# Scores of two blocks in one stretch, softmax written behind the older values, one PSUM tile for both streams

## The chip, the cores and the metric

The kernel runs on one core of one Trainium2 chip. The metric is the device time of one execution in microseconds, as the median of several runs. A core has four computing engines that run beside each other, each with a queue of its own: TensorE (PE, with its weight loads PEld), VectorE (DVE), ScalarE (ACT) and GpSimd (POOL). SyncE (SP) issues the DMAs. TensorE writes only to PSUM, of which a core has eight banks of 512 float32 values per partition; the kernel divides all eight among three kinds of buffers.

## The reference

Two layers over 1024 tokens of width 1024, each of the form x + rmsnorm(mixer(rmsnorm(x))). Layer 0 is a gated multi-scale retention with 8 heads. Layer 1 is a gated differential attention, 8 heads, which is where the change lies:

```python
def block(args):
    q_i, i = args
    q_chunk = (i * Q_BLOCK + jnp.arange(Q_BLOCK)) // CHUNK
    mask = key_chunk[None, :] <= q_chunk[:, None]
    sc = jnp.einsum('bqhtd,bkhtd->bhtqk', q_i.astype(jnp.float32), kf) * scale
    p = jax.nn.softmax(jnp.where(mask, sc, neg), axis=-1)
    w = p[:, :, 0] - lam * p[:, :, 1]
    return jnp.einsum('bhqk,bkhe->bqhe', w, vf)
```

Each head has two streams t of queries and keys, 64 wide each. A block of 128 queries sees the keys up to its own chunk of 64, so block b needs 128 (b + 1) keys, of which the upper half of the queries alone sees the last 64. The two softmaxes are combined with the weight lam, multiplied with the values (128 wide), normed per head, gated, projected and normed again.

## The kernel before, in words

Everything is float32 in and out. A product of two matrices is made of three matmuls (helper `mm3`, its matmul on L100): each factor is split into a rounded high part and a low remainder (`split`, L87 and L88, or L90 and L91 with a scale), and high x high, high x low and low x high are summed in PSUM.

Layer 0 runs first: projections, retention and an output product, until about 850 us of the span. Then come the gates of layer 1, then its 64 units of projection, 8 heads (h) of 8 chunks of 128 tokens (c). This main loop, index i = 8 h + c, is the place of the change. One step of it projects chunk c of head h to queries, keys and values: eight slabs s, three matmuls of 128x384 each (`gemm_piece`, tile `pg`). Between the slabs other work is written:

- `ahead`: weights of a later head are fetched and split (L90, L91; tile `wbh`), one slab in each of the steps c = 1 to 4 and four in step c = 7;
- at s = 4, `transpose_b` turns the previous chunk's rotated queries and keys (L582 on TensorE, then L87 and L88);
- behind the odd slabs s = 1, 3, 5, 7, one of the "pieces" that the generator `attend` yields, two steps late (`LAG`).

At the end of a step `rotate_b` applies the rotary angles (L571, L572 on DVE, L573 on POOL) and copies the values (L574 on ACT).

A unit of attention is one head and one block b. It passes through three functions in three successive steps:

- `scores`: for each 512 keys, three matmuls for each of the two streams (L596). Stream t uses the rows 64 t to 64 t + 63 of queries and keys, so these matmuls work on half of the array's height each and the two streams run as a pair. Then, in the same function, softmax: a memset that masks the last 64 keys (L602), a maximum (L603), both on DVE, an exponential with its sum on ACT (L604), and on DVE the reciprocal, the weight and the combination of the two streams (L606, L607, L609).
- `turn`: transposes of the combined weights, up to four into one PSUM buffer (L621), and a copy on ACT (L622); two pieces for more than 512 keys.
- `values`: two instructions of TensorE for each key block (L632), then ACT reads the sum out (L635) and squares it (L636), a reciprocal root follows (L105 on DVE, L106 on POOL), the product on POOL (L638), and a DMA stores the block (L639).

So a step that scores unit k also values unit k - 2 and turns unit k - 1, in the written order scores with softmax, values, turn, turn.

PSUM buffers come from three tags: `g`, two of one bank (projections and output products); `s2`, two of two banks (1024 values; one for each stream of a unit); `s`, two of one bank (transposes, turns and values in rotation). SBUF tag `k` has six buffers of 1024 values, for softmax weights (`pr`), turned weights (`wT`) and rows of the output product.

The order on each engine is not simply the written one: a planner takes instructions by priority in the written order among those that are ready by its own clock of the engines, gives out buffers, and puts in the waits. What it has ordered, each engine runs in turn.

Behind the main loop, the remaining pieces of `attend` are woven with the output product: four of its steps (three matmuls of 128x512 each, `out_gemm`) stand ahead of the last `transpose_b`; then each of the remaining pieces is followed by three more. `out_fetch(t)` reads block t of the attention back from DRAM, when its eight heads are stored, multiplies it with the gate (L672), and `out_turn` transposes it (L680).

Of the kernel before, what the change touches and what calls it, by code (L numbers as in the profile page):

```python
# [18 lines left out]
P = 128  # L19
D = 1024  # L20
S = 1024
NC = S // P
NS = D // P
H = 8
# [11 lines left out]
def yoco_kernel(ctx: ExitStack, tc: tile.TileContext, a: dict):  # L36
# [31 lines left out]
    def kt(shape, nm, dt=F32):  # L68
        return sbuf("k", shape, dt, nm)

    def sm(n):
        return sbuf("m", [P, n], F32, "m")
# [3 lines left out]
    def ps(tag, n=512):  # L76
        return psum.tile([P, n], F32, name=f"p{tag}_{next(uid)}", tag=tag, bufs=PB[tag])
# [327 lines left out]
    for i in range(H * NC):  # L405
        h, c = divmod(i, NC)
        if c == 0:
            wq, wg = w_next
        u = {"h": h, "c": c, "wg": wg, "pp": ps("s2", 1024)}
# [176 lines left out]
    def scores(u):  # L586
        h, b, nk = u["h"], u["b"], u["nk"]
        q, qs = groups[h, b // 4][0][:, 0], slice(b % 4 * P, b % 4 * P + P)
        sc = [ps("s2", 1024) for t in range(2)]
        for c0 in range(0, nk, 512):  # L590
            n = min(512, nk - c0)
            k = groups[h, c0 // 512][0][:, 1]
            for i, (ql, kl) in enumerate(((0, 0), (0, 1), (1, 0))):
                for t in range(2):
                    rows = slice(t * 64, t * 64 + 64)
                    nc.tensor.matmul(  # L596
                        sc[t][:, c0 : c0 + n], q[rows, ql, qs], k[rows, kl, 0:n], start=(i == 0), stop=(i == 2)
                    )
        nm, s_ = sm(2), sm(2)
        pr = [kt([P, D], f"pr{t}") for t in range(2)]  # L600
        for t in range(2):
            nc.vector.memset(sc[t][0:64, nk - 64 : nk], NEG)  # L602
            nc.vector.tensor_reduce(out=nm[:, t : t + 1], in_=sc[t][:, :nk], axis=AX.X, op=ALU.max, negate=True)  # L603
# [34 lines left out]
        nc.gpsimd.tensor_tensor(out=o[:, 1], in0=o[:, 0], in1=r.to_broadcast([P, P]), op=ALU.mult)  # L638
        nc.sync.dma_start(og2d[b * P : (b + 1) * P, h * P : (h + 1) * P], o[:, 1])  # L639

    def attend(blocks):

        blocks = [{"h": h, "b": b, "nk": (b + 1) * P} for h, b in blocks]
        a_, b_ = None, None
        for u in blocks + [None, None]:
            pieces = []
            if u:
                pieces.append(lambda: scores(u))
            if a_:
                pieces.append(lambda: values(a_))  # L650
            if b_:
                pieces.append(lambda: turn(b_, 0))
                if b_["nk"] > 512:
                    pieces.append(lambda: turn(b_, 1))
            yield pieces
            a_, b_ = b_, u


    wob = {}
# [64 lines left out]
                yield  # L724

    LAG = 2
    att = attend([(h, b) for h in range(H) for b in range(NC)])
    prev = None
    for i in range(H * NC):
        h, c = divmod(i, NC)  # L730
# [24 lines left out]
        load_wob(f, wt([P, D], "wobh"), wt([P, D], "wobl"))  # L755
    spare = xt([P, 512], "spare", F32)
    og_ = outs()
    for _ in range(4):
        next(og_)
    transpose_b(*prev)  # L760
    for step in att:
# [91 lines left out]
```

## Time and profile before

| what | us |
|---|---|
| median of 3 runs (1496.89 to 1499.78) | 1497.07 |
| the profiled execution | 1498.85 |
| its span, from first to last instruction | 1496.8 |
| TensorE busy | 1478.4 |
| VectorE busy | 787.2 |
| ScalarE busy | 629.3 |
| GpSimd busy | 269.9 |
| scores on TensorE (L596), first to last start | 937.0 to 1401.4 |

Rows of a profile name the line, the engine, the operation, the tile written and the tile read, the shape (rows x columns of the array for TensorE, partitions x elements), and a count. In a group's row the two numbers behind the bar are the busy time in us and the mean of one in ns, then the idle time of the engine just before and what ended it. A row of the timeline begins with the start in us from the first instruction and the length of the merged run in us. TensorE's matmuls overlap: the next starts before the modelled end of the one before, so a run is measured from start to start.

### The profile page before, as it was taken

How to read it: one execution, taken by the hardware profiler on the slowest of the kernel's cores; microseconds unless marked ns; L12 is line 12 of the kernel's file. 1: busy time of each engine (PE TensorE's matmuls, PEld its weight loads, DVE VectorE, ACT ScalarE, POOL GpSimd, SP SyncE). 2: the span in 40 equal slices, each digit the busy share in tenths (PEclk: the TensorE clock that was granted, in tenths of full speed). 3: DMA queues.
4: the chain of work that ended last, by engine and by line, in shares of the span. 5: the costliest groups of instructions: out<-in, count | busy, mean ns of one | idle time of the engine just before them, and what ended most of it. 6: DMA issues, size and time to landing. Idle time of an engine off the chain costs nothing.

```text
span 1496.8 us, 23855 instructions
## 1 busy us (share of the span) xinstructions
PE 1478.4 (99%) x8770; PEld 1296.9 (87%) x8770; DVE 787.2 (53%) x1991; ACT 629.3 (42%) x1611; POOL 269.9 (18%) x470
## 2 busy tenths in 40 slices
PE   9999999999999999999999999999999999999998
PEld 7889888989889898888888888988988988988786
DVE  5764635454545454541155502667567576577543
ACT  5642424242424332342244513556455566466421
POOL 1322222222122222200000000122222222222100
PEclk9999999999999999999999999999999999999999
DMA  7530303020211111253445522111011011013342
GB/s 259 169 113 15 95 15 99 15 89 22 81 33 56 58 65 53 71 180 105 141 159 179 183 71 79 31 36 52 12 52 52 10 52 48 15 64 139 122 166 98
DMA packets 71173, 125.63 MB, mean 84 GB/s; under 512 B 7697, under 2 KB 42385, under 8 KB 71057
## 3 DMA queue, kind: packets, MB, share of 16 engines
q1 hardware_dynamic: 70768, 123.85, 25.3%
q8 instruction: 69, 1.13, 0.3%
q14 instruction: 48, 0.39, 0.1%
q10 hardware_dynamic: 288, 0.26, 0.1%
HBM read 94.72 MB, written 29.36 MB: 83 GB/s over the span
## 4 chain that ended last, share of the span: by engine, by line
PE 86%; DVE 5%; ACT 3%; issue 2%; DMA 2%; POOL 0%; DVEq 0%; POOLq 0%; ACTq 0%; SPq 0%
PE pg L100 58%; PE ps L100 14%; PE ps L596 4%; PE ps L632 3%; PE ps L621 2%; DMA stg<-in_wa 1%; PE ps L304 1%; ACT pr L604 1%; DVE wbh L91 1%; PE ps L254 1%; PE ps L582 1%; DVE m L603 1%; DVE wq L91 0%; PE ps L238 0%; PE ps L680 0%
## 5 line engine op out<-in xcount | busy, mean ns | idle before, releaser
L100 PE MATMUL pg<-wq,xT 128*128 128x512 f32 x1512 | 378.5, 399 | 1.1 <-ACT xT L87 0.5
L100 PE MATMUL pg<-wbh,x2T 128*128 128x384 f32 x1536 | 334.9, 353 | 0.0
L100 PEld LDWEIGHTS pg<-wq,xT 128*128 128x128 f32 x1512 | 274.7, 188 | 55.6 <-ACT wq L90 1.1
L100 PEld LDWEIGHTS pg<-wbh,x2T 128*128 128x128 f32 x1536 | 256.2, 189 | 13.0 <-issue 9.3
L100 PE MATMUL ps<-wg,xT 128*128 128x256 f32 x1536 | 195.8, 283 | 0.1
L100 PEld LDWEIGHTS ps<-wg,xT 128*128 128x128 f32 x1536 | 189.4, 192 | 0.7 <-DVE wg L91 0.3
L106 POOL TENSOR_TENSOR m<-m,mhalf 128x1 f32<-128x1 f32 x144 | 79.9, 555 | 572.7 <-DVE m L105 485.2
L604 ACT ACTIVATE pr<-ps,m 128x256 f32<-128x256 f32 (+7 forms) x128 | 94.1, 738 | 90.9 <-DVE m L603 90.9
L221 POOL TENSOR_TENSOR a<-a 128x256 f32<-128x256 f32 x64 | 48.2, 753 | 327.7 <-DVE a L220 321.8
L603 DVE TENSOR_REDUCE m<-ps 128x1 f32<-128x256 f32 (+7 forms) x128 | 91.1, 753 | 0.0
L100 PE MATMUL pg<-wbg,x2T 128*128 128x512 f32 x384 | 88.4, 390 | 0.0
L90 ACT ACTIVATE r<-pg,tabA 128x256 fp32r<-128x256 f32 x63 | 29.7, 471 | 134.0 <-DVE a L220 133.9
L100 PEld LDWEIGHTS pg<-wbg,x2T 128*128 128x128 f32 x384 | 71.8, 188 | 14.8
L100 PEld LDWEIGHTS ps<-r,r 128*128 128x128 f32 x528 | 72.1, 190 | 7.3 <-ACT r L256 1.5
L255 DVE TENSOR_TENSOR a<-ps,tabA 128x128 f32<-128x128 f32 x64 | 18.6, 290 | 112.0 <-PE ps L254 111.3
L100 PE MATMUL ps<-r,r 128*128 128x256 f32 x528 | 74.8, 284 | 1.0 <-ACT r L256 0.7
L632 PE MATMUL ps<-v,wT 128*128 128x128 f32 x576 | 74.6, 275 | 0.2 <-DVE ps L602 0.2
L632 PEld LDWEIGHTS ps<-v,wT 128*128 128x128 f32 x576 | 73.2, 191 | 0.7 <-PE pg L100 0.5
L573 POOL TENSOR_TENSOR tabB<-tabB 128x256 f32<-128x256 f32 x64 | 49.6, 775 | 124.9 <-DVE tabB L572 124.7
L219 DVE TENSOR_TENSOR a<-pg,tabA 128x256 f32<-128x256 f32 x63 | 26.6, 423 | 79.2 <-PE pg L100 79.2
L256 ACT ACTIVATE r<-a 128x128 fp32r<-128x128 f32 x64 | 19.9, 310 | 107.8 <-DVE a L255 107.8
L100 PE MATMUL pg<-wo,oh 128*128 128x512 f32 x192 | 60.8, 398 | 1.1 <-ACT oh L87 1.1
(158 smaller groups left out, 2387.2 us busy)
## 6 DMA issues: line engine op xcount, KB each, us to landing
stw<-in_wa SPq DMA_DIRECT2D x56, 256.0 KB, 2.8
stb<-in_wbh SPq DMA_DIRECT2D x64, 192.0 KB, 2.4
xr<-in_x SPq DMA_DIRECT2D x16, 512.0 KB, 4.4
stg<-in_wa SPq DMA_DIRECT2D x32, 256.0 KB, 3.3
ogd<-a SPq DMA_DIRECT2D x64, 128.0 KB, 1.9
sto<-in_woa SPq DMA_DIRECT2D x16, 512.0 KB, 3.7
og<-ogd SPq DMA_DIRECT2D x16, 512.0 KB, 4.0
y0d<-y SPq DMA_DIRECT2D x8, 512.0 KB, 2.7
```

What stands on the lines that cost most here:

```text
L90: nc.scalar.activation(hi, src, AF.Copy, scale=scale)
L100: nc.tensor.matmul(out, l, r, start=(first and i == 0), stop=(last and i == n - 1))
L106: nc.gpsimd.tensor_tensor(out=out, in0=t, in1=mhalf[:, 0:n], op=ALU.pow)
L219: nc.vector.tensor_tensor(out=o4(t1), in0=q4, in1=cb, op=ALU.mult)
L221: nc.gpsimd.tensor_tensor(out=qk, in0=t1, in1=t2, op=ALU.add)
L256: nc.scalar.activation(ss[:, 0, :], sc, AF.Copy)
L573: nc.gpsimd.tensor_tensor(out=r[:, 2], in0=r[:, 0], in1=r[:, 1], op=ALU.add)
L596: nc.tensor.matmul(sc[t][:, c0 : c0 + n], q[rows, ql, qs], k[rows, kl, 0:n], start=(i == 0), stop=(i == 2))
L603: nc.vector.tensor_reduce(out=nm[:, t : t + 1], in_=sc[t][:, :nk], axis=AX.X, op=ALU.max, negate=True)
L604: nc.scalar.activation(pr[t][:, :nk], sc[t][:, :nk], AF.Exp, bias=nm[:, t : t + 1], accum_out=s_[:, t : t + 1])
L621: nc.tensor.transpose(pt[:, k - k0 : k - k0 + P], w[:, k : k + P], ident)
L632: nc.tensor.matmul(po, wT[:, kb * P : (kb + 1) * P], v[:, kb % 4], start=(kb == 0), stop=(kb == b))
```

## The change

Score matmuls and softmax become two functions. The generator no longer walks over units but over 66 steps: within a head, steps 0 and 2 score nothing, step 1 scores blocks 0 and 1 one after the other, step 3 blocks 2 and 3, and steps 4 to 7 one block each. The softmax of the units just scored is written in the second piece, behind the values of older units; units scored together are turned together in the next step and valued together in the one after. A unit of up to 512 keys takes one `s2` buffer in place of two, stream 0 in the first 512 columns and stream 1 in the last, and likewise one `k` buffer for its softmax weights. Behind the main loop six steps of the output product in place of four stand ahead of the last `transpose_b`.

```diff
     def scores(u):
         h, b, nk = u["h"], u["b"], u["nk"]
         q, qs = groups[h, b // 4][0][:, 0], slice(b % 4 * P, b % 4 * P + P)
-        sc = [ps("s2", 1024) for t in range(2)]
+        if nk > 512:
+            sc = [ps("s2", 1024) for t in range(2)]
+        else:
+            both = ps("s2", 1024)
+            sc = [both[:, t * 512 : t * 512 + 512] for t in range(2)]
         for c0 in range(0, nk, 512):
...
+        u["sc"] = sc
+
+    def softmax(u):
+        nk, sc = u["nk"], u["sc"]
         nm, s_ = sm(2), sm(2)
-        pr = [kt([P, D], f"pr{t}") for t in range(2)]
+        if nk > 512:
+            pr = [kt([P, D], f"pr{t}") for t in range(2)]
+        else:
+            both = kt([P, D], "pr")
+            pr = [both[:, t * 512 : t * 512 + 512] for t in range(2)]
         for t in range(2):
             nc.vector.memset(sc[t][0:64, nk - 64 : nk], NEG)
...
-    def attend(blocks):
-
-        blocks = [{"h": h, "b": b, "nk": (b + 1) * P} for h, b in blocks]
-        a_, b_ = None, None
-        for u in blocks + [None, None]:
+    def attend():
+        scored, turned = [], []
+        for i in range(H * NC + 2):
+            h, b = divmod(i, NC)
+            new = [] if h == H or b in (0, 2) else [b - 1, b] if b in (1, 3) else [b]
+            new = [{"h": h, "b": k, "nk": (k + 1) * P} for k in new]
             pieces = []
-            if u:
-                pieces.append(lambda: scores(u))
-            if a_:
-                pieces.append(lambda: values(a_))
-            if b_:
-                pieces.append(lambda: turn(b_, 0))
-                if b_["nk"] > 512:
-                    pieces.append(lambda: turn(b_, 1))
+            if new:
+                pieces.append(lambda: [scores(u) for u in new])
+            pieces.append(lambda: [values(u) for u in turned] + [softmax(u) for u in new])
+            for u in scored:
+                pieces.append(lambda u=u: turn(u, 0))
+                if u["nk"] > 512:
+                    pieces.append(lambda u=u: turn(u, 1))
             yield pieces
-            a_, b_ = b_, u
+            scored, turned = new, scored
...
-    att = attend([(h, b) for h in range(H) for b in range(NC)])
+    att = attend()
...
     og_ = outs()
-    for _ in range(4):
+    for _ in range(6):
         next(og_)
     transpose_b(*prev)
```

## The prediction

> **What bounds the kernel now.** I read the page first (busy shares, then the chain that ended last), then the stretch of the attention heads in windows, TensorE's own timeline there, and last the list of what TensorE waits for.
>
> ```profile
> PE 1478.4 (99%) x8770; PEld 1296.9 (87%) x8770; DVE 787.2 (53%) x1991; ACT 629.3 (42%) x1611; POOL 269.9 (18%) x470
> PE 86%; DVE 5%; ACT 3%; issue 2%; DMA 2%; POOL 0%; DVEq 0%; POOLq 0%; ACTq 0%; SPq 0%
> ...
> 1111.00:1169.00 58.00, 57.45 (x389) 51.59 (x388) 37.91 (x104) 32.62 (x100) 13.43 (x24) 1.00 0.12 37
> ```
>
> TensorE is busy for 99% of the span and holds 86% of the last chain. The third row is one head (58.00 us; columns are the busy time of PE, PEld, DVE, ACT and POOL, then the granted clock 1.00, the DMA share and GB/s): DVE works 37.91 us and ACT 32.62 of it, so neither is a bound on average. The head costs what TensorE's order of instructions costs, plus the moments in which it waits. So I price the change on TensorE's timeline, and look at DVE and ACT only for lateness.
>
> The busy figure hides something, since ends of matmuls are modelled. Starts show it. These are TensorE's runs (start, length, what, count) around the scores of one head's block 0 (128 keys), block 1 (256), block 3 (512) and block 4 (512 + 128 keys):
>
> ```profile
> 1106.26 1.29 PE L100 MATMUL pg<-wbh,x2T 128*128 128x384 f32 x6
> 1107.49 0.55 PE L596 MATMUL ps<-qk 64*128 64x128 f32 x6
> 1107.97 1.31 PE L100 MATMUL pg<-wbh,x2T 128*128 128x384 f32 x6
> 1109.12 1.72 PE L632 MATMUL ps<-v,wT 128*128 128x128 f32 x14
> ...
> 1113.80 1.31 PE L100 MATMUL pg<-wbh,x2T 128*128 128x384 f32 x6
> 1115.04 0.63 PE L596 MATMUL ps<-qk 64*128 64x256 f32 x6
> 1115.60 1.33 PE L100 MATMUL pg<-wbh,x2T 128*128 128x384 f32 x6
> 1116.76 1.95 PE L632 MATMUL ps<-v,wT 128*128 128x128 f32 x16
> ...
> 1125.63 2.36 PE L100 MATMUL pg<-wbh,x2T 128*128 128x384 f32 x12
> 1127.93 0.96 PE L596 MATMUL ps<-qk 64*128 64x512 f32 x6
> 1128.82 1.31 PE L100 MATMUL pg<-wbh,x2T 128*128 128x384 f32 x6
> 1129.97 0.61 PE L632 MATMUL ps<-v,wT 128*128 128x128 f32 x4
> ...
> 1131.07 0.77 PE L100 MATMUL pg<-wbh,x2T 128*128 128x384 f32 x3
> 1131.68 0.49 PE L621 MATMUL ps<-ident,pr 128*128 128x128 f32 x3
> 1131.93 2.33 PE L100 MATMUL pg<-wbh,x2T 128*128 128x384 f32 x12
> 1134.19 0.96 PE L596 MATMUL ps<-qk,qk 64*128 64x512 f32 x6
> 1134.99 0.45 PE L596 MATMUL ps<-qk 64*128 64x128 f32 x6
> 1135.37 1.34 PE L100 MATMUL pg<-wbh,x2T 128*128 128x384 f32 x6
> 1136.54 0.83 PE L632 MATMUL ps<-v,wT 128*128 128x128 f32 x6
> ```
>
> A projection matmul takes about 0.175 us: 1125.63 with twelve against 1106.26 with six differ by 2.30 - 1.23 = 1.07 for six, 0.178 each; 1131.07 to 1131.68 gives 0.61 for three, that is 3 x 0.175 and 0.085 for following a transpose run. Each score stretch (L596: two row halves of 64, so 64*128) can now be priced from the start of the projection run before it to the start of the value matmuls behind it, less the projection matmuls between, less 0.085:
>
> - 128 keys: 2.86 - 12 x 0.175 - 0.085 = 0.675 us
> - 256 keys: 2.96 - 2.10 - 0.085 = 0.775
> - 512 keys: 4.34 - 18 x 0.175 - 0.085 = 1.105
> - 512 and 128 keys in one stretch: 4.61 - 3.15 - 0.085 = 1.375
>
> The last is the key: 512 and 128 keys apart cost 1.105 + 0.675 = 1.78, joined 1.375. Entering and leaving a stretch of half-height matmuls costs 0.40 us, and the joined second part adds only 0.27.
>
> **The waits.** In the heads TensorE waits little:
>
> ```profile
> PE ps L621 <- ACT o L635: 4.8, 9, 0.9
> PE ps L582 <- POOL tabB L573: 0.7, 1, 0.7
> ```
>
> (in total, times, longest). The first comes about once a head, in the step that scores block 6. There the rows are:
>
> ```profile
> 1151.20 1.28 PE L632 MATMUL ps<-v,wT 128*128 128x128 f32 x10
> ...
> 1152.84 1.01 ACT L604 ACTIVATE pr<-ps,m 128x896 f32<-128x896 f32 x1 [1.93 <-DVE m L603]
> ...
> 1152.97 0.77 PE L100 MATMUL pg<-wbh,x2T 128*128 128x384 f32 x3
> ...
> 1153.84 0.36 ACT L635 ACTIVATE o<-ps,m 128x128 f32<-128x128 f32 x1
> ...
> 1154.25 0.66 PE L621 MATMUL ps<-ident,pr 128*128 128x128 f32 x4 [0.51 <-ACT o L635]
> ...
> 1155.62 0.41 DVE L88 TENSOR_TENSOR qk<-ps,qk 128x256 fp32r<-128x256 f32 x1
> ...
> 1155.95 1.14 DVE L609 SCALAR_TENSOR_TENSOR pr<-pr,m,pr 128x896 f32<-128x896 f32 x1
> ```
>
> The last of ten value matmuls starts near 1152.2 (0.11 us apiece: 1.28 less 0.28 for the last, over nine), but their read-out (L635) stands in ACT's queue behind the exponential that began at 1152.84, so it starts at 1153.84; the transposes (L621) need its PSUM buffer. From 1152.97 to 1154.25 are 1.28 us where 0.61 are due: 0.67 lost, 0.51 of it shown as idle. Also to be seen: DVE runs L88, written later in the program, ahead of L609. The engines' queues are the planner's, by readiness, with the written order as priority.
>
> **The change, part by part.**
>
> *Joined scores.* Matmul counts stay. Per head blocks 0+1 and 2+3 join, so two entries and exits fall away: 16 over 8 heads. At 0.40 that is 6.4 us. Both ends: low 0.30 (the 128-key stretch at 0.675 less all of the 0.38 from 1134.99 to 1135.37), high 0.46 (rounding of four starts, 0.01 to 0.02 each): 4.8 to 7.4. I take 0.40, the pair that the trace itself shows joined. No cover is needed: TensorE is the bound.
>
> *Softmax behind the older values.* Memset, reduction, exponential and L609 are now written after the value matmuls, so L635, L636 and L105 have priority. This can take away the L635 waits: 4.8 us idle, 4.8 x 0.67/0.51 = 6.3 in starts. In the rows above the values end only some 0.4 us ahead of the exponential's start (1151.20 + 1.28 = 1152.48 against 1152.84), and the planner takes whatever its own clock says is ready; I take half, 3.0 (bounds 0 and 6.3). What is late next there is L88 (1155.62), which frees the buffer of the second transpose piece.
>
> *Six output steps ahead of the last transpose instead of four.* Six more output matmuls stand before L582, more than 6 x 0.175 = 1.05 us, which covers the 0.7 us wait: 0.7 gained, bounds 0 and 0.9.
>
> *One tile for both streams, values and turns in pairs.* Steps 1 and 3 now carry two units, steps 0 and 2 none. New dependences: (a) block 4's scores need both PSUM tiles, which blocks 2 and 3 hold; (b) after the paired values, the projection's transposes need the first value buffer; (c) step 2 is short. The work that must be hidden in (a):
>
> ```profile
> L604 ACT ACTIVATE pr<-ps,m 128x512 f32<-128x512 f32 x16 | 10.9, 684 | 13.3 <-DVE m L603 13.3
> L604 ACT ACTIVATE pr<-ps,m 128x384 f32<-128x384 f32 x16 | 9.2, 577 | 10.9 <-DVE m L603 10.9
> L604 ACT ACTIVATION_READ_ACCUMULATOR pr<-ps,m 128x1 f32 x128 | 25.1, 196 | 0.0
> L635 ACT ACTIVATE o<-ps,m 128x128 f32<-128x128 f32 x64 | 23.4, 365 | 25.0 <-issue 20.7 <-PE ps L632 4.3
> L636 ACT ACTIVATE o<-o 128x128 f32<-128x128 f32 x64 | 20.1, 314 | 0.6
> L87 ACT ACTIVATE qk<-ps 128x256 fp32r<-128x256 f32 x63 | 24.1, 383 | 2.0 <-PE ps L582 2.0
> ```
>
> Four exponentials 2 x (0.68 + 0.58) and their four read-outs of about 0.1 net: 2.9. Two values 2 x (0.37 + 0.31 + 0.1) = 1.6, L87 0.4: 4.9 us on ACT if all of it goes first. TensorE in that time: 24 projection matmuls 4.2, two transposes 0.2, six value matmuls (0.11 each) 0.7: 5.1. So it just fits; the end of block 3 is covered only if ACT has no holes. I put 0.1 us a head for (a) to (c) together, 1.0 in all with a little for step 5 (bounds 0 and 1 us a head, as one wait of today is at most 0.9). The last head's block 0 is stored one step later, so the first output fetch starts later; its transposes wait for nothing now:
>
> ```profile
> L680 PE MATMUL ps<-ident,og 128*128 128x128 f32 x64 | 9.6, 272 | 0.0
> ```
>
> I put 0.5 once (0 to 1.3). DMAs are the same in number.
>
> A rule of the Trainium skill speaks against the shared tile: TensorEngine Tiling (Array Packing), Gotcha 1: PSUM Pressure, says that different row tiles cannot access the same PSUM bank at once. By it, two streams in one bank would have to run one after the other; PSUM - Partial Sum Buffer, Specifications, gives 512 FP32 values to a bank, so the offset of 512 puts them in two. It makes a rival below.
>
> *Sum.* -6.4 - 3.0 - 0.7 + 1.0 + 0.5 = -8.6. The profiled execution took 1498.85 (span 1496.8 and 2.05 around it); less 8.6 that is 1490.2. The median of the runs, 1497.07, lies 1.8 below the profiled one, so I forecast 1488.5.
>
> **Rivals.**
>
> *All waits go* (14%). Then 6.4 + 6.3 + 0.9, and nothing new: -13.6, 1483.5. For it: L635 is written first. Against: DVE is late there as well.
>
> *PSUM held at block 4* (13%). ACT order leaves holes between exponentials, or one tile for two streams makes memset and exponential of the two halves follow each other. At 0.6 us a head 4.8 are given back: 1493.3. Against it: 4.9 fits into 5.1.
>
> *The stretch isn't joined* (8%). The planner puts projection matmuls between the two units because a buffer is not free by its clock; the change does not do what it says: -8.6 + 6.4, 1494.9. Against: both tiles were read a step earlier.
>
> *Softmax starts late* (6%, slower). If the planner keeps the written order on DVE, the reductions of steps 5, 6 and 7 wait for L105, which waits for the values: two slabs (1.05), the values (1.1 for ten), L635 and L636 with what lies between (0.9): about 3 us, where today they need only the scores. L88 then comes 3 us later, and the second transpose piece with it. Three steps x 8 heads x 3 = 72, less 8.6: 1560. It decides from 8.6/24 = 0.36 us of delay a step. Against: L88 ahead of L609 shows that order is by readiness. The Trainium skill (PSUM - Partial Sum Buffer, Engine vs sequencer instructions) says that these queues are strict FIFO; by it, a head waiting in the planned order would indeed hold all behind it.
>
> *Streams no longer side by side* (3%, slower). If the two halves in one tile went one after the other, each of the 12 pairs a head would cost a second matmul, 0.11 (128 keys) to 0.23 (512), 3 x (0.11 + 0.12 + 0.175 + 0.23) = 1.9 us with the two middle sizes set between, 15.2 in all: 1503.7. Against: the offset is one full matmul width of 512.
>
> **How the numbers follow.** The forecast has 56%; its own range is 1485.5 to 1491.5. Range: down to 1482 for the waits, up to 1495 for held PSUM and the stretch not joined; the two slower cases (9%) and a part of the first rival stay out. A change of 0.2% is 3 us, about what can be told here from none. Faster: 56 + 14 + 9 of the 13 + 3 of the 8 = 82%; same 9%; slower 9%.
>
> **What would show it.** L596 in 48 runs instead of 64 (joined runs of 128, 256 and 384, 512), each join worth 0.40 in starts; L621 waiting less on L635; L582 no longer waiting once; no new row for L596 waiting on ACT. Wrong if new waits of L582, L621 or L596 sum to more than 5 us.

## The result and the profile after

The change made the kernel slower. Its median is 1515.95 us (1515.24 to 1516.02) against 1498.42 us of the kernel before (1496.89 to 1499.99), a ratio of 1.0119 with a 95% interval of 1.0107 to 1.0131. The forecast was 1488.5, in a range from 1482 to 1495. The profiled execution of the changed kernel took 1515.24 us (span 1513.5), 16.4 more than the profiled one before.

New line numbers: scores L600, memset L614, reduction L615, exponential L616, combination L621, transposes of weights L633 and their copy L634, values L644, their read-out L647 and square L648, transposes of the output rows L695.

The busy shares and the chain that ended last, of the changed kernel:

```profile
PE 1499.0 (99%) x8770; PEld 1316.4 (87%) x8770; DVE 782.3 (52%) x1991; ACT 633.8 (42%) x1611; POOL 266.0 (18%) x470
...
PE 89%; DMA 3%; DVE 3%; ACT 1%; issue 1%; POOL 0%; POOLq 0%; DVEq 0%; SPq 0%; ACTq 0%
```

The same 58 us window as before the change (busy PE, PEld, DVE, ACT, POOL, then the granted clock):

```profile
1111.00:1169.00 58.00, 57.89 (x374) 52.01 (x373) 35.64 (x102) 32.04 (x96) 12.42 (x22) 1.00 0.12 37
```

It has 374 matmuls where 389 stood, at the same clock. With as many instructions as before in the whole, TensorE is busy for 20.6 us more (1478.4 before), and VectorE and ScalarE hold less of the chain than before (3% and 1%, where they held 5% and 3%). Nothing looks like a wait. What TensorE waits for in the heads shrank:

```profile
PE ps L633 <- DVE pr L621: 1.0, 3, 0.5
PE ps L633 <- DVE wo L88: 0.7, 1, 0.7
PE ps L600 <- ACT pr L616: 0.6, 1, 0.6
PE ps L633 <- DVE ps L614: 0.3, 1, 0.3
```

The 4.8 us for the value read-outs and the 0.7 us for L573 are gone. The loss stands in the groups by shape (count, busy time, mean ns of one). First before, then after:

```profile
L596 PE MATMUL ps<-qk,qk 64*128 64x512 f32 x192 | 30.8, 425 | 0.0
```

```profile
L600 PE MATMUL ps<-qk,qk 64*128 64x512 f32 x192 | 51.7, 428 | 0.6 <-ACT pr L616 0.6
```

One matmul takes what it took, 425 and 428 ns, yet 192 of them fill 51.7 us in place of 30.8: they no longer overlap. TensorE's timeline in one head shows which ones (blocks 0 and 1, then block 4):

```profile
1057.03 2.33 PE L100 MATMUL pg<-wbh,x2T 128*128 128x384 f32 x12
1059.29 0.96 PE L600 MATMUL ps<-qk 64*128 64x128 f32 x12
1060.18 1.31 PE L100 MATMUL pg<-wbh,x2T 128*128 128x384 f32 x6
1061.33 1.95 PE L644 MATMUL ps<-v,wT 128*128 128x128 f32 x16
...
1079.82 0.96 PE L600 MATMUL ps<-qk,qk 64*128 64x512 f32 x3
1080.61 0.44 PE L600 MATMUL ps<-qk 64*128 64x128 f32 x3
1080.99 0.44 PE L100 MATMUL pg<-wbh,x2T 128*128 128x384 f32 x1
...
1082.25 1.29 PE L100 MATMUL pg<-wbh,x2T 128*128 128x384 f32 x6
1083.47 0.96 PE L600 MATMUL ps<-qk,qk 64*128 64x512 f32 x3
1084.27 0.44 PE L600 MATMUL ps<-qk 64*128 64x128 f32 x3
1084.64 1.32 PE L100 MATMUL pg<-wbh,x2T 128*128 128x384 f32 x6
1085.80 0.63 PE L633 MATMUL ps<-ident,pr 128*128 128x128 f32 x4
```

Blocks 0 and 1 stand in one stretch (x12), as meant. Block 4 stood in one stretch of 6 + 6 before; now it is two stretches of 3 + 3, one for each stream, 3.65 us apart, with other work between. The second, priced as the prediction priced stretches (1082.25 to 1085.80 = 3.55, less 12 x 0.175, less 0.085), costs 1.365 us. The pair of both streams cost 1.375. A stream alone costs what both cost side by side.

**All stretches counted.** For the tables below I took the starts of all TensorE instructions from the first matmul on `wbh` (about 927 us) to TensorE's last start. A score stretch is charged from the start of the instruction ahead of it to the start of the second one behind it, less the usual lengths of the two neighbours (0.175 for a projection matmul, 0.11 for the others, 0.23 for the output product). Every other gap above the usual length goes to "waits and the rest". The usual lengths sum to 473.15 us in every run, so the two columns carry the whole difference on TensorE. A wait inside a score stretch, or at its edge, counts with the scores. Two matmuls count as a pair if they start within 16 ns.

| per head, us | before | after |
|---|---|---|
| blocks 0 and 1 | 0.679 + 0.755 | 1.083 |
| blocks 2 and 3 | 0.921 + 1.093 | 1.622 |
| block 4 | 1.375 | 2.737 |
| block 5 | 1.448 | 2.989 |
| block 6 | 1.686 | 2.077 |
| block 7 | 1.791 | 2.076 |
| all scores, 8 heads | 77.98 | 101.32 |
| waits and the rest, 8 heads | 11.90 | 6.33 |

Scores cost 23.3 us more, waits 5.6 less: +17.7, less 1.2 by which the part before the heads was shorter, against 16.7 between the spans. The joins gave 5.9 (8 x 0.74), and the torn blocks 4 to 7 took 28.6 (8 x 3.58); 0.6 are a block 3 that fell apart once. Of 576 score matmuls 338 start without a partner; before, 2.

**How a pair is torn.** VectorE and ScalarE in the same head, between the scores of blocks 2 and 3 and those of block 5:

```profile
1073.32 0.11 DVE L614 MEMSET ps<- 64x64 f32 x1 [0.58 <-PE ps L600]
...
1075.62 0.15 DVE L105 TENSOR_SCALAR m<-m 128x1 f32<-128x1 f32 x1 [2.18 <-ACT o L648]
...
1076.31 0.15 DVE L105 TENSOR_SCALAR m<-m 128x1 f32<-128x1 f32 x1 [0.54 <-ACT o L648]
1076.38 0.55 DVE L615 TENSOR_REDUCE m<-ps 128x1 f32<-128x384 f32 x1
...
1076.96 0.58 ACT L616 ACTIVATE pr<-ps,m 128x384 f32<-128x384 f32 x1 [0.42 <-DVE m L615]
...
1077.99 0.11 DVE L614 MEMSET ps<- 64x64 f32 x1
...
1078.91 0.58 ACT L616 ACTIVATE pr<-ps,m 128x384 f32<-128x384 f32 x1
...
1082.45 0.69 ACT L616 ACTIVATE pr<-ps,m 128x512 f32<-128x512 f32 x1 [0.38 <-DVE m L615]
```

Three things are to be seen. By 1073.32 the first stream of both blocks was masked, but VectorE stands idle until two L105 of the older values have run; the first reduction starts 3 us late. Within a tile for two streams the second stream's memset comes only after the first stream's exponential, so one unit takes 2.53 us from its first reduction (1076.38) to the start of its last exponential (1078.91); VectorE runs L88, L571 and L572 in between. Before, with a tile for each stream, the two reductions of the same block ran in a row and this took 1.16:

```profile
1064.88 1.02 DVE L603 TENSOR_REDUCE m<-ps 128x1 f32<-128x384 f32 x2
...
1065.47 0.58 ACT L604 ACTIVATE pr<-ps,m 128x384 f32<-128x384 f32 x1 [1.36 <-DVE m L603]
...
1066.04 0.57 ACT L604 ACTIVATE pr<-ps,m 128x384 f32<-128x384 f32 x1
```

And so block 2's tile comes free at 1079.49 and block 3's at 1083.14. Stream 0 of block 4 starts at 1079.82 and stream 1 at 1083.47, each right behind the tile that it needs.

### The profile page after: what moved, and what is told of

The parts are those of the page before. It is cut to its first block, busy times and chain, and to the rows that moved or that the text cites. A ratio compares the mean times of both kernels' runs of the same rounds, so it can differ in the third digit from the quotient of the medians.

```text
span 1513.5 us, 23824 instructions
## 1 busy us (share of the span) xinstructions
PE 1499.0 (99%) x8770; PEld 1316.4 (87%) x8770; DVE 782.3 (52%) x1991; ACT 633.8 (42%) x1611; POOL 266.0 (18%) x470
## 4 chain that ended last, share of the span: by engine, by line
PE 89%; DMA 3%; DVE 3%; ACT 1%; issue 1%; POOL 0%; POOLq 0%; DVEq 0%; SPq 0%; ACTq 0%
PE pg L100 59%; PE ps L100 14%; PE ps L600 5%; PE ps L644 4%; PE ps L633 2%; PE ps L304 1%; DMA stg<-in_wa 1%; PE ps L582 1%; PE ps L254 1%; DMA g<-gd 1%; PE ps L238 0%; DVE wq L91 0%; DMA sto<-in_wob 0%; PE ps L239 0%; PE ps L695 0%
## 5 line engine op out<-in xcount | busy, mean ns | idle before, releaser
L100 PE MATMUL pg<-wbh,x2T 128*128 128x384 f32 x1536 | 324.1, 350 | 0.0
L616 ACT ACTIVATE pr<-ps,m 128x256 f32<-128x256 f32 (+7 forms) x128 | 94.4, 739 | 57.4 <-DVE m L615 55.3
L615 DVE TENSOR_REDUCE m<-ps 128x1 f32<-128x256 f32 (+7 forms) x128 | 93.7, 748 | 0.8
L573 POOL TENSOR_TENSOR tabB<-tabB 128x256 f32<-128x256 f32 x64 | 48.0, 750 | 256.6 <-DVE tabB L572 237.2
L90 ACT ACTIVATE r<-pg,tabA 128x256 fp32r<-128x256 f32 x63 | 29.6, 471 | 134.3 <-DVE a L220 133.9
L100 PEld LDWEIGHTS pg<-wbg,x2T 128*128 128x128 f32 x384 | 71.8, 188 | 14.8
L644 PE MATMUL ps<-v,wT 128*128 128x128 f32 x576 | 73.5, 277 | 0.0
L644 PEld LDWEIGHTS ps<-v,wT 128*128 128x128 f32 x576 | 70.1, 191 | 3.0 <-ACT wT L634 1.8
L647 ACT ACTIVATE o<-ps,m 128x128 f32<-128x128 f32 x64 | 23.3, 365 | 115.8 <-issue 76.5
L105 DVE TENSOR_SCALAR m<-m 128x1 f32<-128x1 f32 x88 | 13.4, 153 | 108.3 <-ACT o L648 101.2
```

Source lines behind the costliest of these rows:

```text
L90: nc.scalar.activation(hi, src, AF.Copy, scale=scale)
L100: nc.tensor.matmul(out, l, r, start=(first and i == 0), stop=(last and i == n - 1))
L573: nc.gpsimd.tensor_tensor(out=r[:, 2], in0=r[:, 0], in1=r[:, 1], op=ALU.add)
L616: nc.scalar.activation(pr[t][:, :nk], sc[t][:, :nk], AF.Exp, bias=nm[:, t : t + 1], accum_out=s_[:, t : t + 1])
L644: nc.tensor.matmul(po, wT[:, kb * P : (kb + 1) * P], v[:, kb % 4], start=(kb == 0), stop=(kb == b))
L647: nc.scalar.activation(o[:, 0], po, AF.Copy, scale=rc[:, 0:1])
```

## The experiments

Each row compares with runs of the kernel before on the same chip.

| run | us | ratio, 95% interval | stretches | without partner | scores | waits, rest | one head |
|---|---|---|---|---|---|---|---|
| before | | | 64 | 2 | 78.0 | 11.9 | 58.28 |
| after | 1515.95 | 1.0107 to 1.0131 | 67 | 338 | 101.3 | 6.3 | 60.49 |
| e1 | 1508.91 | 1.0058 to 1.0088 | 48 | 84 | 79.6 | 22.3 | 59.44 |
| e2 | 1508.06 | 1.0051 to 1.0081 | 60 | 260 | 93.5 | 5.3 | 59.25 |
| e3 | 1510.42 | 1.0066 to 1.0096 | 56 | 122 | 82.4 | 20.1 | 60.00 |
| e4 | 1506.49 | 1.0030 to 1.0063 | 66 | 10 | 81.6 | 15.8 | 58.31 |
| e5 | 1517.04 | 1.0109 to 1.0139 | 57 | 108 | 85.3 | 21.2 | 59.79 |
| e6 | 1505.77 | 1.0033 to 1.0063 | 48 | 0 | 71.5 | 24.8 | 58.78 |
| e7 | 1499.45 | 0.9993 to 1.0011 | 48 | 72 | 72.8 | 17.7 | 58.27 |
| e8 | 1506.07 | 1.0037 to 1.0071 | 71 | 150 | 92.0 | 5.4 | 58.83 |
| e9 | 1505.12 | 1.0029 to 1.0057 | 65 | 6 | 78.0 | 16.2 | 58.89 |
| e10 | 1499.35 | 0.9991 to 1.0010 | 48 | 2 | 71.2 | 17.6 | 58.32 |
| e11 | 1501.74 | 1.0006 to 1.0026 | 48 | 36 | 72.9 | 19.8 | 58.64 |
| e12 | 1501.59 | 1.0008 to 1.0027 | 49 | 96 | 76.7 | 18.2 | 58.56 |
| e13 | 1504.09 | 1.0022 to 1.0043 | 49 | 84 | 76.4 | 17.4 | 58.42 |
| e14 | 1504.39 | 1.0018 to 1.0042 | 48 | 108 | 76.3 | 17.3 | 58.47 |
| e15 | 1503.24 | 1.0018 to 1.0039 | 49 | 106 | 78.3 | 16.0 | 58.48 |
| e16 | 1501.22 | 1.0000 to 1.0019 | 48 | 88 | 71.8 | 19.5 | 58.64 |
| e17 | 1506.31 | 1.0030 to 1.0060 | 61 | 314 | 91.8 | 5.6 | 59.05 |

The last column is the median of heads 1 to 6, each from its first projection matmul to that of the next head. It leaves out the first head, the last one and the output product, where a single long wait can weigh as much as a change in all heads. No version shortens a head by more than 0.01 us against the kernel before.

The expectations of e1 to e4 count torn matmuls by the names of tiles; a tile for two streams has one name, so whole pairs were counted as torn there (the 33 stretches of e4 above all). The table counts by starts.

### e1 to e3: one edit each in the changed kernel

e1 writes softmax directly behind the scores again:

```diff
-                pieces.append(lambda: [scores(u) for u in new])
-            pieces.append(lambda: [values(u) for u in turned] + [softmax(u) for u in new])
+                pieces.append(lambda: [scores(u) for u in new] + [softmax(u) for u in new])
+            pieces.append(lambda: [values(u) for u in turned])
```

> The changed kernel with one line undone: the softmax stands in the first piece, right behind the scores, and the values have the second piece for themselves. Joined stretches, the one tile, six output steps stay. In the order that it was given all 48 score stretches hold both streams (the changed kernel: 34 stretches with one stream alone). Theory P (the loss is the tall units' streams run one after the other): the tearing goes, 16 joins at 0.40 remain, waits as before or fewer: 1485 to 1493, against 1498.4 before and 1516 changed. Rival T (the loss is the one tile for both streams, whose second memset waits for the first exponential, and stays): above 1508. Rival J (joined stretches delay something else): above 1498.

e2 writes both memsets ahead of both reductions:

```diff
         for t in range(2):
             nc.vector.memset(sc[t][0:64, nk - 64 : nk], NEG)
+        for t in range(2):
             nc.vector.tensor_reduce(...)
```

> The changed kernel with both memsets of a unit written ahead of both reductions, so no memset waits for an exponential on the same tile. 20 stretches with one stream (113 matmuls) instead of 34 (194) in the order given. Theory P: the loss goes with the torn matmuls; of about 23 us (17.5 lost in all and 6 gained by joins) the share 113/194 stays: about 1506. Rival T: the memset is the whole cause, below 1493. If the late softmax alone counts, by waits of TensorE and not by tearing: unchanged, 1514 to 1517.

e3 gives the small tiles of the softmax a tag of their own, where they shared 48 buffers with those of values and norms:

```diff
-        nm, s_ = sm(2), sm(2)
+        nm, s_ = sm2(2), sm2(2)
...
-        rc, cf = sm(2), sm(1)
+        rc, cf = sm(2), sm2(1)
```

> The changed kernel with the softmax's small tiles (maxima, sums, weight) in a tag of their own, so that they need not be handed out behind those of the values written ahead of them; 16 stretches with one stream (96 matmuls). If the written order holds the reductions back through the shared tag: the first reductions of steps 3 to 7 start ahead of L105 and the time falls with the torn matmuls, by P to about 1498.4 - 6 + 23 x 96/194 = 1504. If L105 ahead of the reductions is of no account: 1514 to 1517.

In e1 blocks 5 to 7 are whole again (1.447, 1.620 and 1.791 a head) and only block 4 is torn (2.39): scores fall from 101.3 to 79.6. But its first theory, 1485 to 1493, missed by 16 us, since it left the waits as they were, and the waits that the change had taken away come back:

```profile
PE ps L633 <- ACT o L647: 4.8, 7, 1.0
PE ps L582 <- ACT o L647: 2.6, 8, 0.4
PE ps L695 <- DVE og L687: 2.4, 1, 2.4
PE ps L582 <- POOL tabB L573: 1.9, 2, 1.4
```

The time, 1508.9, is in the ranges of both rivals. Rival J has the cause of these waits; the shared tile of rival T can't be the whole loss, since it is still there and scores fell by 21.7.

e3 does the same by another way (82.4 and 20.1), and at 1510.4 also misses its forecast of 1504. e2 mends little of the tear (260 partners lost) and keeps the waits low; its 1508.1 lies near the 1506 of theory P, and rival T, below 1493, is out. So lateness of softmax is what tears most pairs, and the waits are low only while it is late: in the runs with a late softmax (after, e2, e5, e8, e17) the transposes of weights wait 0.2 us at most for the values' read-out; in those with a prompt one they wait 2.5 to 8.1, in the kernel before 4.8.

### e4, e8 and e9: single parts put into the kernel before

e4 takes the shared tiles alone (the two `if nk > 512` of the change), e8 the written place of softmax alone, e9 is e8 with e3's own tag:

```diff
-            if a_:
-                pieces.append(lambda: values(a_))
+            if a_ or u:
+                pieces.append(lambda: [values(x) for x in (a_,) if x] + [softmax(x) for x in (u,) if x])
```

> The kernel before with one part of the change alone: one PSUM tile and one SBUF tile for both streams up to 512 keys; no joined stretches, softmax where it was. 33 stretches with one stream (193 matmuls). Theory P: nothing is gained and all that tearing costs is paid: 1498.4 + 22 = about 1520 (1514 to 1526). If the tearing costs nothing and the late softmax does it: 1497 to 1501.

> The kernel before with one part of the change alone: the softmax is a function of its own, written behind the values of the older unit in the same step; two tiles a unit, no joins. If the late softmax alone makes tiles come free late and apart, the order given tears some pairs (54 matmuls of 576): about 54/228 of the 29 us that the changed kernel pays, 7 us, less up to 5 us of waits for L635 taken away: 1496 to 1504. If the written order is of no account: 1497 to 1500 with the same waits as before.

> e8 (softmax written behind the older values, nothing else of the change) with the softmax's small tiles in a tag of their own; 2 torn matmuls in the order given instead of e8's 54. Theory S (the late softmax tears pairs only because its first small tile is handed out behind those of the values, so its reduction queues behind L105 on VectorE): the stretches fall back from 92 to 78 us and the time from 1506 to 1492 to 1500, by how many of the waits for L635 stay away. If the shared tag is of no account: 1504 to 1508.

e8 tears pairs without any shared tile or join: 150 lost partners, scores +14.0 (2.8 of it are waits of score matmuls for an exponential), waits -6.5, +7.6 us in time, more than the 1504 at which its forecast ended.

e4 took 1506.5, neither the 1520 of theory P nor 1497 to 1501. It tears almost none (10), and heads 1 to 6 take what they took before (58.31 and 58.28). Its loss falls in the last head, most of it in one wait of 4.1 us:

```profile
PE ps L629 <- ACT o L643: 8.1, 8, 4.1
```

There ScalarE waits 6.00 us for the DMA of an output weight (`sto`, L90), and the next exponentials and the read-out L643 stand behind it. Block 5 of that head, cut by transposes of output rows, costs 3.93; in the seven others it costs 1.45. So the shared tile costs a head next to nothing as long as a step scores one block.

Why softmax is late, VectorE shows behind the scores of block 2, first e8, then e9:

```profile
1066.46 0.19 DVE L606 MEMSET ps<- 64x64 f32 x2 [0.40 <-PE ps L596]
1068.77 0.15 DVE L105 TENSOR_SCALAR m<-m 128x1 f32<-128x1 f32 x1 [2.12 <-ACT o L640]
1068.84 1.01 DVE L607 TENSOR_REDUCE m<-ps 128x1 f32<-128x384 f32 x2
```

```profile
1067.69 0.19 DVE L609 MEMSET ps<- 64x64 f32 x2 [0.99 <-PE ps L599]
1067.84 1.02 DVE L610 TENSOR_REDUCE m<-ps 128x1 f32<-128x384 f32 x2
```

In e8 VectorE idles 2.12 us with masked scores before it and runs L105 first; in e9, where only the tag differs, the reduction follows the memset at once, and scores fall back to 78.0. Sharing the tag is the cause of the late start. The reading that fits, not shown by itself, is that a tag's buffers are handed out in the written order: the memset needs none, the reduction writes one, and the values' small tiles are written ahead of it. e9 also shows the other side. Its stretches came as theory S said, its time, 1505.1, as the rival said: with softmax prompt the waits are 16.2, though softmax is still written behind the older values:

```profile
PE ps L628 <- ACT o L642: 7.0, 7, 2.1
PE ps L628 <- ACT wT L629: 3.1, 7, 1.2
```

The first row is the wait for the values' read-out, 4.8 in the kernel before. The written place alone does not take it away.

### e5 to e7: a tie between the two streams

Ahead of the scores of blocks with over 512 keys, a 1 x 1 memset writes into stream 1's buffer and a 1 x 1 copy carries it into stream 0's, so neither stream can start before both are free:

```diff
         if nk > 512:
             sc = [ps("s2", 1024) for t in range(2)]
+            nc.vector.memset(sc[1][0:1, 0:1], 0.0)
+            nc.vector.tensor_copy(sc[0][0:1, 0:1], sc[1][0:1, 0:1])
```

e5 is the changed kernel with the tie, e6 adds e1's edit, e7 adds e3's instead.

> The changed kernel with one addition: for a block above 512 keys a 1x1 memset of stream 1's PSUM tile and a 1x1 copy of it into stream 0's tile stand ahead of the score matmuls, so that neither stream's matmuls can be placed until both tiles are free. Theory P (the loss is the streams run one after the other because their two tiles come free apart): score stretches fall from 101.3 us in TensorE's starts to 72 to 76, waits rise a little: 1486 to 1496. Rival H (block 4's scores are late whatever their form, because the tile of block 3 is held by its softmax; what is saved on the stretches comes back as waits of TensorE for L616): stretches as in P, but waits up by 10 us or more: 1502 to 1516.

> The tie of e5 and the softmax back behind the scores, as in e1. All 48 stretches paired in the order given. Against e1 (1508.9) the ten torn matmuls of each block 4 go, 8 us by e1's trace (2.46 against 1.44 us from start to start, 8 heads). P: 1499 to 1502, the rest of the loss being the waits that e1 shows for L582, L633 and L695. H: 1506 to 1510.

> The tie of e5 and the softmax's small tiles in a tag of their own, as in e3. All 48 stretches paired. Against e3 (1510.4) some 17 us of stretches go (89.9 to 72). P with e3's waits: about 1494 (1489 to 1500). H: above 1504.

e6 has every pair whole and shows the joins by themselves: 48 stretches, 71.5 us against 78.0. Its block 4:

```profile
1078.91 0.96 PE L602 MATMUL ps<-qk,qk 64*128 64x512 f32 x6
1079.71 0.45 PE L602 MATMUL ps<-qk 64*128 64x128 f32 x6
```

But it waits 24.8 us in all; its 1505.8 is almost that of rival H (1506 to 1510), not theory P's 1499 to 1502. And e5, where softmax is late and the tie makes TensorE wait for it, is no faster than the change:

```profile
PE ps L602 <- ACT wT L636: 7.3, 7, 1.1
PE ps L582 <- ACT o L649: 4.1, 14, 0.4
PE ps L697 <- ACT wT L636: 3.8, 1, 3.8
PE ps L602 <- DVE ps L592: 2.0, 1, 2.0
```

The first row is block 5. It names L636 as what came last, but the tie's copy (L592) is late there too: in one head it ends at 1088.24, and the scores start at 1088.38. e5's 1517.0 is a little above rival H's range, and far from theory P's 1486 to 1496.

e7 has the tie and the tag of its own, and is level with the kernel before: scores 5.2 less, waits 5.8 more. Its 1499.5 lies at the upper end of theory P's range, 1489 to 1500. Against e3 its scores fell by 9.6, not by 17: the 89.9 of the expectation is 82.4 in the count used here. The tie keeps stretches in one piece, but not every start: in e7 72 matmuls begin over 16 ns from their partner, 70 of them in block 5, and why is not shown.

### e10 and e11: the waits of e7 attacked

e10 is e7 with the values of the second of two paired blocks one piece later; e11 adds e2's order and the first transposes of the output rows four slabs later.

```diff
+            if turned[1:] and not scored:
+                pieces.append(lambda: values(turned[1]))
             for u in scored:
-                pieces.append(lambda u=u: turn(u, 0))
+                pieces.append(lambda u=u: [values(v) for v in turned[1:]] + [turn(u, 0)])
...
-            if i == H * NC - 1 and s in (0, 2):
-                out_turn(0, s // 2)
+            if i == H * NC - 1 and s in (4, 6):
+                out_turn(0, s // 2 - 2)
```

> e7 (tie and own tag) with the values of the second unit of a pair one piece later than those of the first. If e7's wait of L582 (0.47 us a head, 3.8 in all) comes from two value buffers taken at once, it goes: 1494 to 1497 against e7's 1499.4, with no L582 waiting for the values' read-out. If the wait is ScalarE's lateness in itself, it moves to another row: 1498 to 1501.

> e10, with the memsets of both streams ahead of both reductions (as e2) and the first output transposes four slabs later. By the accounts of TensorE's starts: joins -6 against the kernel before, no tearing, waits of 8 to 12 us as before or less: 1488 to 1494. If the memsets do not matter without tearing and the output transposes find another wait: 1494 to 1498.

In e10 the gaps ahead of the transposes of queries and keys fell from 5.9 to 0.5 us, those ahead of the transposes of weights rose from 6.1 to 10.8: the waits moved, as e10's second forecast said (1498 to 1501). In a middle head e10's scores cost 8.89 us in place of 9.76, and the waits 2.19 in place of 1.27. e11, at 1501.7, is slower than either of its forecasts (1488 to 1498).

### e12 to e17: the inner order of softmax

e12 is e1 with e2. e13 is e12 with the two edits of e10 and e11 quoted above; e14 is e13 with the tie. In e15 to e17 a unit does both memsets, then both reductions, then both exponentials: e15 in e1, e16 in e7, e17 in the changed kernel.

```diff
         for t in range(2):
             nc.vector.memset(sc[t][0:64, nk - 64 : nk], NEG)
+        for t in range(2):
             nc.vector.tensor_reduce(...)
+        for t in range(2):
             nc.scalar.activation(...)
```

> The changed kernel with two edits: softmax written directly behind the scores again (as in e1) and both masking memsets written ahead of both reductions (as in e2). No tie. Theory (a unit's pair of streams is torn when its two PSUM buffers come free apart; in e1 only block 4 is still torn, because in a tile for two streams the memset of one half waits for the exponential of the other, and so block 3's buffer comes free 2 to 3 us behind block 2's): with the memsets first, the two exponentials of a tile follow the reductions without a memset between, so the buffers come free closer together, and block 4 should lose 2 partners a head in place of 10. Score stretches fall from e1's 79.6 us to about 72, so 7 to 8 us below e1's 1508.9: about 1501, with e1's waits (22 us) as they are. Rival (block 4 is torn whatever the order of the memsets, because blocks 2 and 3 are simply two tiles with two softmaxes): as e1, 1509, 80 unpaired matmuls.

> e12 with two more edits: the values of the second of two paired blocks written one piece later, and the first transposes of the last output product four slabs later. Theory (with pairs whole, what keeps the joined scores from paying is waits behind paired values): e6, the same with a tie, had 5.8 us of waits of the transposes of rotated queries and keys behind the paired values' read-out, which the spread took away in e10, and 2.4 us of waits for the first output block, which are shown once. About 1501 less 2.4 and less up to 5.8: 1493 to 1499; under 1495 it would be faster than the kernel before. Rival (a wait taken away at one place comes back at another, as e10 and e11 did: turns wait for the read-outs of the later values): no better than e12 less the 2.4, 1498 to 1501.

> e13 with the tie of e5 (a 1 x 1 memset and a 1 x 1 copy ahead of the scores of blocks with over 512 keys, so that neither stream starts before both buffers are free). No matmul loses its partner, score stretches at 71.5 us. It tells apart, against e13, whether a wait for both buffers costs more than two torn matmuls a head. Theory: two torn matmuls cost 2 x 0.2 us a head, 3 us in all, less than the tie's two small instructions on VectorE and its wait: 0 to 4 us slower than e13. Rival (a torn pair costs more than its missing partners, since it comes as a stretch of its own with entry and exit): 3 to 6 us faster than e13.

> The changed kernel with the softmax directly behind the scores (as e1), and within a unit both memsets, then both reductions, then both exponentials (e12 has the memsets first, but each reduction still followed by its exponential). In e12's trace the second reduction of a tile for two streams starts at 1071.35, only after the exponential of the other stream (1070.64 to 1071.22), though both only read, and though the memsets were done; in the kernel before, with a tile for each stream, the two reductions run in a row (1.02 us for both). Theory (two engines that touch one PSUM tile are kept in the written order, even if both only read and read different halves): with both reductions written first, the second no longer waits, the first reduction to the last exponential's start of a unit of 384 keys takes about 1.7 us in place of e12's about 1.9 and the 2.1 of e6; two units of a head together come free 0.3 to 1 us sooner, and the time falls to 1499 to 1501 from e12's 1501.6. Rival (the wait is not between readers of the tile but one for an engine that is busy elsewhere): the second exponential is as late as in e12, 1501.6.

> e7 (tie, small tiles of the softmax in a tag of their own, softmax behind the values; 1499.45, 17.7 us of waits, 72.8 us of score stretches) with both reductions of a unit ahead of both exponentials. Theory: shorter chains of softmax let the buffers come free earlier; the two tiles' transposes of weights come earlier and wait less, 1 to 3 us in all: 1496 to 1498.5, which would put it level with the kernel before or just under it. Rival (e7's waits are for value read-outs on ScalarE, L652, which the order within a softmax does not change): 1499.5.

> The changed kernel with nothing but both memsets, then both reductions, then both exponentials of a unit (e2 with one more step). The planned order of TensorE shows 61 stretches of scores. If the order between readers of a shared tile is what frees the two buffers of block 4 apart, fewer partners are lost than in e2 (260, score stretches 93.5 us): at 0.085 us for each lost partner (93.5 less 71.5 over 260) some 150 lost ones make 84 us, and about 1499 in place of e2's 1508. Rival (the tear comes from the softmax being late, whatever its inner order): as e2, 1506 to 1508.

e12 took 1501.59, the time of its first theory, but partly by luck: block 4 lost 92 partners, not 16, scores came to 76.7, not 72, and the waits to 18.2, not 22. The streams of block 4 are interleaved, but start 129 to 185 ns apart, and cost 1.514 a head in place of e1's 2.39, 7.0 in all. Block 5 costs 1.45 in seven heads as before and 5.46 in the last, where the first transposes of output rows fall into its stretch and wait:

```profile
PE ps L696 <- DVE og L688: 3.0, 1, 3.0
```

In e2 and e12 the second reduction of a shared tile still starts after the first exponential; the planned order of e12 gives it a wait for ScalarE and for nothing else, though both only read, each its own half. These are the two reductions of block 2 in head 0, from the program as built, with the semaphores that they wait for:

```
L616 TENSOR_REDUCE m_9196<-ps_1355_9182 128x1 [waits DVE_49]
L616 TENSOR_REDUCE m_9196<-ps_1355_9182 128x1 [waits Activation_49]
```

In that order all 32 second reductions of a shared tile wait for ScalarE, and none of the 64 reductions of blocks with a tile for each stream does, though these share their small tile of maxima in the same way. With both reductions written first (e15) the wait is gone:

```profile
1069.33 1.02 DVE L616 TENSOR_REDUCE m<-ps 128x1 f32<-128x384 f32 x2
...
1070.38 0.58 ACT L618 ACTIVATE pr<-ps,m 128x384 f32<-128x384 f32 x1 [2.02 <-DVE m L616]
...
1070.95 0.57 ACT L618 ACTIVATE pr<-ps,m 128x384 f32<-128x384 f32 x1
```

First reduction to last exponential's start is 1.62 us, against 2.53 in the changed kernel. The theory was right on the chain (1.7 forecast) and wrong on what it is worth: e15 is not faster than e12, e16 not faster than e7, both outside their forecasts, and e17, with softmax still late, loses 314 partners and takes 1506.3, as its rival said. e13 took 1504.1, more than the 1493 to 1501 of its theory and rival. e14's time is level with e13's, within its theory's 0 to 4 us, but of its pairs, which the tie should keep whole, 108 matmuls start apart.

So with softmax prompt the order within a shared tile is worth the tear of block 4 (e1 to e12), and the further step to e15 nothing; with softmax late (e2, e17) most of the tear stays whatever that order. When softmax starts weighs more.

No version is faster than the kernel before; e7 and e10 can't be told from it.

## Why the prediction was wrong

**Joined scores (-6.4, bounds 4.8 to 7.4): right.** The joins of blocks 0 and 1 save 0.351 a head, those of blocks 2 and 3 save 0.392, 5.9 in all; with next to no pair torn, e6 and e10 save 6.5 and 6.8.

**Softmax behind the values (-3.0, bounds 0 to 6.3): the number came, but not for the reason given.** The waits for L635 went, and the whole column fell by 5.6 in the change and 6.5 in e8, so the rival "all waits go" had this size right. But the sum took the written place as the cause, and a gain that stands by itself. In e9, with the same written place and a prompt softmax, the waits for the read-out are 7.0. They are gone only where softmax starts late, and that lateness is also what tears the pairs: gain and loss came together.

**Six output steps (-0.7): the wait for L573 is gone in the changed kernel;** in e1 and e6 it is back with 1.9, so six steps alone do not cover it. **First fetch later (+0.5):** no wait for it shows in the changed kernel; in e1 it is 2.4 and in e12 3.0, above the bound of 1.3.

**The step that failed is new dependence (a):** "block 4's scores need both PSUM tiles, which blocks 2 and 3 hold", priced with (b) and (c) at 0.1 us a head, with 1 us a head as the bound, since "one wait of today is at most 0.9". The dependence was seen, but it was priced as a wait. The planner does not wait: it takes what is ready, so it issues stream 0 when block 2's tile is free and stream 1 when block 3's is. The price is a second stretch, 1.37 us, for block 4 and, since the streams stay apart, for block 5, and parts of that for 6 and 7: 3.58 us a head, 28.6 in all. Of the 16.7 us between the spans, heads 0 to 6 hold 15.6 and what comes before and behind them the rest.

The sum of ScalarE's work (4.9 into 5.1 us) was also wrong in its premise. It set 2.9 us for the four exponentials, without holes, and let them begin behind the scores. In the rows above the first begins at 1076.96, 3.5 us behind the masking, and the last ends at 1083.14: 6.2 us for four of them, since in a shared tile memset and reduction of one half wait for the other half's exponential and VectorE has other work between.

**The rivals.** Four of them named parts of this, each with another end. "Softmax starts late" (6%) had the reductions wait for L105, as they do, but priced it through L88 at 72 us; what it did was to tear pairs. The argument against it, that L88 ran ahead of L609, says nothing of a reduction that waits for a small buffer. "PSUM held at block 4" (13%) had memset and exponential of the two halves follow each other, as they do, at 0.6 us a head. "Streams no longer side by side" (3%) put the loss into the shared tiles of short blocks; in the changed kernel these start 2 to 7 ns apart, and it is the blocks with a tile for each stream that lost their partners. "The stretch isn't joined" (8%) came nearest: the planner splits a stretch because a buffer is not free by its clock. It looked for this between two units, where the joins came, and priced it as the gain that stays away. None asked what the planner does when only one of two streams can go.

The Trainium skill's TensorEngine Tiling (Array Packing), Tiling Modes, says that different tiles of the array work in parallel. The trace agrees and shows both ends: 1.375 us a head for block 4 with both streams at once, 2.737 with one after the other.

**What was asked for as evidence:** scores in 48 runs were forecast, 67 were seen; the sign named for a failure, new waits of over 5 us, did not come. A loss that looks like work was not on the list.

**Left open.** The 16 to 25 us of waits in versions with a prompt softmax, against 11.9 before, move from place to place (e10, e13, e14). e9 has 16.2 without valuing two blocks at once, so this is not their only source; how much of them it makes was not settled.

## What to carry to other kernels

When two instructions run fast only because they stand beside each other, ask of a change not only whether a buffer comes later, but whether the two buffers still come free together: an order made by readiness tears the pair rather than wait, and the profile books the loss as busy time with unchanged mean lengths. Look for it in the count of stretches and in starts, not in waits. Look at single heads too: a mean over eight hides whether all lost a little or the last one a lot. Before moving work behind other work in the written order, check which small buffers the two share.

## What the runs showed of the hardware and the planned order

- Half-height matmuls of two streams start 2 to 7 ns apart when paired (blocks 0 to 3 of the changed kernel), and the second stream costs nothing (block 4: 1.375 us for both, 1.365 for one). Where only the order is paired but the first start is off, as in e12's block 4, the offset stays through the three pairs of 512 keys (137 ns in most heads) and the block costs 0.14 us more, not a whole stretch.
- Two engines that read different halves of one PSUM tile are kept in the written order by a wait, although the halves are 512 values, one bank, apart. The Trainium skill's PSUM - Partial Sum Buffer, PSUM bank collisions raise a hardware error, tells of a compiler that orders two engines' accesses to one bank and 32-partition quadrant, reads too; in this case the order goes by tile: 2.53 us for a unit's softmax chain against 1.16 with a tile for each stream in the kernel before, 1.62 with the order changed.
